# Values of two attention groups made once for eight heads with 512-column products, instead of twice for four heads with 256-column ones

## The chip, the cores and the metric

The kernel runs on one core of a Trainium2 chip. The metric is the device time of one launch in microseconds (us). All arithmetic is on fp32 data. TensorE (PE) multiplies, VectorE (DVE) and ScalarE (ACT) do the elementwise work, GpSimd (POOL) a little of it, and SyncE (SP) issues the DMAs between memory and SBUF.

## The reference, cut to what matters

There are 1024 tokens of width 1024 and two layers. Layer A is an mLSTM mixer. Layer B is dilated window attention with 8 heads of width 128 and three groups `g`, whose dilations are 1, 4 and 16; keys and values of all groups come from layer A's normalised output `x`.

```python
x = layer_norm(ALPHA * x + mlstm_layer(x, ...), ln_g[0], ln_b[0])
kv = (x @ w_kv).reshape(bsz, s, 2 * N_GROUPS_B, HEADS_B, HEAD_DIM_B)
for g, (window, dilation) in enumerate(GROUPS_B):       # (128,1), (512,4), (2048,16)
    kb, vb = blocks(kv[:, :, 2 * g]), blocks(kv[:, :, 2 * g + 1])
    o, lse = dilated_block_attention(qb, kb, vb, dilation, window // dilation, slopes)
wts = softmax(stack(lses), axis=0)
o = sum(wts[..., None] * stack(outs), axis=0)
y = (o * silu(z)) @ w_out
x = layer_norm(ALPHA * x + y, ln_g[1], ln_b[1])
```

The values of a group are `x` (1024 x 1024) times a 1024 x 1024 part of `w_kv`: 128 columns for each of the 8 heads.

## The kernel before

**Products.** An fp32 product is three TensorE matmuls over a high and a low part of each operand (`mm3`, lines 97, 98 and 99). `split` makes the parts: ACT casts the high one (L92), DVE subtracts it from the source for the low one (L93). Large products are Strassen's seven products of quarters. `operands` holds x in quarters "11", "12", "22" and sums "s1" to "s4", each made (by adds, L141) and split when it is first asked for. `strassen_steps` yields between its products, so that the caller can put other work there.

**Layer A's end.** The last output rows are normalised, transposed on TensorE (`transposes`, L1012) and evicted to SBUF with gain and shift (ACT at L1018, DVE at L1016). The last four of eight row blocks are handled by `self.a_last`, which `layer_b` calls inside its first product.

**Layer B.** Heads go in two quads, 0 to 3 and 4 to 7; for each quad the groups 0, 1, 2. For a quad and a group, `values` comes first, then for each head `queries_keys` (a Strassen product of 84 matmuls of 512 columns), `scores`, `head_values` (splits of the head's values) and `attend` (P times V). After group 2 a head's three outputs are merged: `merge` works out per-token weights in rows of 8 partitions (L1360 to L1379) and stores them as "f"; `fetch` loads the outputs and the weights broadcast to 128 partitions (tiles `fbs`); `weigh` calls `combine`, which multiplies and adds tiles of 128x1024 on DVE (L1401, L1403) and multiplies by the gate (L1405). `weigh` of a head runs after the next head's scores; that of head 3 runs inside `values(0, 1)` (argument `beside`).

**Values before.** For groups 0 and 1, `values(g, quad)` makes 4 heads' values, 512 columns. In `strassen_steps` with `tokens`, the stationary operand is 128 tokens of x and the moving one 256 columns of weights; one call is 7 products of 48 matmuls. For group 1 the result is regrouped by a store to memory ("vn") and a load. Group 2 is made in another way (`values_turned`).

**Gates.** `gates(c2)` makes silu gates for two heads of a layer-B column block, a Strassen product of 84 matmuls of 512 columns. `gates(0)` is interleaved with `values(0, 0)`; `gate_at` puts the others ahead of `values` of a (quad, group).

**Order.** A tile scheduler orders the instructions of each engine from the code's order, priorities and the slots (numbered SBUF buffers) that become free; on the chip each engine runs its list in that order.

## Time and profile before

| what | value |
| --- | --- |
| median of 3 runs | 2027.93 us (2026.33 to 2030.51) |
| profiled execution | 2026.42 us, its span from first to last instruction 2024.6 us |
| TensorE busy | 1975.5 us, 98% of the span |
| VectorE busy | 1453.3 us, 72% |
| ScalarE busy | 1014.2 us, 50% |
| mean granted TensorE clock | 0.994 of full speed |

Layer A takes the first 966 us of the span. A granted clock of 1.00 is the higher of TensorE's two levels (2.4 GHz), 0.50 the lower (1.2 GHz). Times within the program are us from the span's start. TensorE's instructions overlap in part, so the time that one adds is the distance between two starts, not its own duration.

### The profile page before, as it was taken

How to read it: one execution, taken by the hardware profiler on the slowest of the kernel's cores; microseconds unless marked ns; L12 is line 12 of the kernel's file. 1: busy time of each engine (PE TensorE's matmuls, PEld its weight loads, DVE VectorE, ACT ScalarE, POOL GpSimd, SP SyncE). 2: the span in 40 equal slices, each digit the busy share in tenths (PEclk: the TensorE clock that was granted, in tenths of full speed). 3: DMA queues.
4: the chain of work that ended last, by engine and by line, in shares of the span. 5: the costliest groups of instructions: out<-in, count | busy, mean ns of one | idle time of the engine just before them, and what ended most of it. 6: DMA issues, size and time to landing. Idle time of an engine off the chain costs nothing. (4 is left out here: it accounts for less than half of the span.)

```text
span 2024.6 us, 28010 instructions
## 1 busy us (share of the span) xinstructions
PE 1975.5 (98%) x10248; PEld 1671.0 (83%) x10248; DVE 1453.3 (72%) x2835; ACT 1014.2 (50%) x1976; POOL 153.3 (8%) x127
## 2 busy tenths in 40 slices
...
DMA packets 113025, 288.15 MB, mean 142 GB/s; under 512 B 13108, under 2 KB 35060, under 8 KB 112888
## 3 DMA queue, kind: packets, MB, share of 16 engines
...
HBM read 200.03 MB, written 86.30 MB: 141 GB/s over the span
## 5 line engine op out<-in xcount | busy, mean ns | idle before, releaser
L97 PE MATMUL b<-s,s 128*128 128x512 f32 (+2 forms) x2944 | 1065.1, 371 | 24.1 <-ACT s L92 20.6
L98 PE MATMUL b<-s,s 128*128 128x512 f32 (+2 forms) x2944 | 1077.7, 367 | 5.2 <-DVE s L93 5.2
L99 PE MATMUL b<-s,s 128*128 128x512 f32 (+2 forms) x2944 | 1063.9, 368 | 4.2 <-DVE s L93 4.1
L92 ACT CAST s<-s 128x512 fp32r<-128x512 f32 (+4 forms) x674 | 435.6, 660 | 534.8 <-PE b L99 276.2
L93 DVE TENSOR_TENSOR s<-s,s 128x512 fp32r<-128x512 f32 (+2 forms) x670 | 507.7, 770 | 250.0 <-ACT s L92 246.8
L97 PEld LDWEIGHTS b<-s,s 128*128 128x128 f32 x2944 | 556.7, 189 | 119.7 <-ACT s L92 27.2
L99 PEld LDWEIGHTS b<-s,s 128*128 128x128 f32 x2944 | 556.9, 190 | 95.5 <-DVE s L93 7.8
L98 PEld LDWEIGHTS b<-s,s 128*128 128x128 f32 x2944 | 557.6, 190 | 92.6 <-DVE s L93 6.8
L230 DVE TENSOR_TENSOR s<-s,b 128x512 f32<-128x512 f32 x168 | 114.6, 683 | 56.3 <-PE b L99 55.0
L1250 ACT ACTIVATE s<-s,nmax 128x128 f32<-128x128 f32 (+1 forms) x192 | 84.7, 444 | 34.4 <-DVE nmax L1248 34.1
L224 DVE TENSOR_TENSOR s<-s,b 128x512 f32<-128x512 f32 x112 | 76.4, 685 | 26.2 <-PE b L99 25.5
L93 DVE TENSOR_TENSOR s<-b,s 128x512 fp32r<-128x512 f32 (+1 forms) x96 | 51.0, 552 | 37.4 <-ACT s L92 33.8
L558 DVE SCALAR_TENSOR_TENSOR s<-s,c_convw,s 128x512 f32<-128x512 f32 (+3 forms) x96 | 71.6, 758 | 3.1 <-ACT s L555 2.8
L243 DVE TENSOR_TENSOR s<-s,s 128x512 f32<-128x512 f32 (+1 forms) x52 | 38.0, 731 | 44.3 <-DMA s<-in_w_xm 14.3
L802 ACT ACTIVATE s<-s,k 128x128 f32<-128x128 f32 x144 | 47.4, 395 | 40.7 <-DVE s L93 18.3
L1246 DVE CUSTOM_DVE_ANT_0 s<-b,k 128x128 f32<-128x128 f32 (+1 forms) x192 | 57.0, 345 | 7.0 <-PE b L99 6.8
L92 ACT CAST s<-b 128x512 fp32r<-128x512 f32 (+1 forms) x96 | 43.5, 481 | 23.9 <-PE b L99 14.2
L1197 DVE SCALAR_TENSOR_TENSOR s<-s,s 128x512 fp32r<-128x512 f32 x48 | 42.4, 885 | 14.7 <-ACT s L1196 14.4
L761 POOL TENSOR_TENSOR s<-s 128x512 fp32r<-128x512 f32 x32 | 43.3, 1365 | 77.1 <-DMA s<-dv 51.3
L872 POOL TENSOR_TENSOR s<-s,s 128x512 f32<-128x512 f32 x32 | 42.3, 1338 | 63.2 <-DVE s L871 51.3
L1326 ACT COPY s<-b 128x512 f32<-128x512 f32 x32 | 36.0, 1124 | 17.6 <-PE b L1287 9.1
L1401 DVE TENSOR_TENSOR s<-s,s 128x1024 f32<-128x1024 f32 (+1 forms) x27 | 29.3, 1103 | 21.5 <-DMA s<-df 21.3
...
## 6 DMA issues: line engine op xcount, KB each, us to landing
...
```

Source lines behind the costliest of these rows:

```text
L92: self.nc.scalar.copy(h, src)
L93: self.last_split = (l_eng or self.nc.vector).tensor_tensor(l, src, f(h), op=ALU.subtract)
L97: mm(ps, lh, rh, start=start, stop=False, skip_group_check=skip)
L98: mm(ps, lh, rl, start=False, stop=False, skip_group_check=skip)
L99: mm(ps, ll, rh, start=False, stop=stop, skip_group_check=skip)
L224: V.tensor_tensor(o, p, q, op=add)
L230: V.tensor_tensor(o, p[lane][rows], q[lane][rows], op=add)
L558: V.scalar_tensor_tensor(u[i][:, lo:o + 512], xm[i][:, lo - s:o + 512 - s], convw[:, c, 3 - s:4 - s], u[i][:, lo:o + 512], op0=ALU.mult, o ...
L761: G.tensor_tensor(l, f(l), f(h), op=ALU.subtract)
L802: A.activation(E[:, i * P:i * P + P], src[:, i * P:i * P + P], AF.Exp, bias=self.bias[:, hd, ig, j:j + 1])
L1246: V.tensor_tensor_reduce(out=dst, in0=sc, in1=bias, op0=ALU.add, op1=ALU.max, scale=1.0, scalar=-3e38, accum_out=mx[:, b:b + 1])
L1250: A.activation(res[b][0], res[b][0], AF.Exp, bias=nm[:, b:b + 1], accum_out=stat[:, 1, g, b:b + 1])
```

## The change

`values(g)` for g = 0 and 1 runs once, at quad 0, for all 8 heads, with `strassen_wide`: the moving operand is 512 columns wide and a result quarter holds 4 heads. A call is again 7 products of 48 matmuls. The half for heads 0 to 3 stays in SBUF; that for heads 4 to 7 is stored to "vn" and loaded at quad 1. For group 1 both halves are regrouped through "vn". `head_values` splits four pieces of 256 columns instead of two of 512. `gates(0)` moves ahead of `values(1, 0)` and `gates(2)` from ahead of `values(1, 1)` to the start of quad 1. `operands` gets spare slots for "s2", and `values(0)` asks for "s2" and "s3" behind the first product and `a_last`. `transposes` takes the columns in another order and `a_last` other PSUM banks. The combine of head 3 is no longer one `weigh` beside values but three steps of `by_group`, one behind the scores of each of heads 4, 5 and 6 of group 0. Only layer B's weights `w_v` are laid out anew for this; the output is the same sum.

```diff
@@ -955,7 +955,7 @@
         lnT = self.const("lnT", [P, 2, KD])
         self.x1 = self.operands(raws, {"11": (4, 5, 6, 7), "12": (8, 9, 10, 11), "22": (0, 1, 2, 3),
                                        "s1": (16, 17, 18, 19), "s2": (20, 21, 22, 23), "s3": (24, 25, 26, 27),
-                                       "s4": (28, 29, 30, 31)}, {})
+                                       "s4": (28, 29, 30, 31)}, {}, spare=(30, 31))
         rs = Ring(44, 45, 46, 52, 13, 47, 48, 49)
         w_raw, whs, wls, yhl = Ring(50, 51), Ring(47, 0, 1, 34), Ring(40, 2, 3, 36), Ring(41, 42, 43, 35)
         rows, stats = {}, {}
...
@@ -1062,7 +1062,7 @@
                     norm((tb - 2, tb - 1, tb))
                 elif i == 3:
                     norm((tb,))
-        self.a_last = lambda: [transposes((4, 5, 6), Ring(2, 3, 4, 5)), transposes((7,), Ring(6, 7))]
+        self.a_last = lambda: [transposes((4, 5, 6), Ring(4, 5, 6, 7)), transposes((7,), Ring(4, 5, 6, 7))]
     def layer_b(self):
@@ -1093,50 +1093,66 @@
             return (dst.rearrange("p (r h i) -> p r h i", r=r, h=2)[:, :, half],
                     src.rearrange("p (i r) -> p r i", r=r))
-        def values(g, quad, beside=None):
+        def values(g, quad):
             if g == 2:
                 return values_turned(quad)
-
-            s0, s1, s2, s3 = vs
-            slots = {(0, 0): s2, (1, 0): s0, (1, 1): s3, (0, 1): s1}
-            vs[:] = s2, s0, s3, s1
-            v = [[None, None], [None, None]]
+            rows = lambda quad, half: self.dram["vn", g, quad, half]
+            natural = lambda ap: ap.rearrange("(t p) n -> p t n", p=P)
+
+            grouped = natural if g == 0 else lambda ap: ap.rearrange("(p r) n -> p r n", r=4)
+            v = [None, None]
+
+            def load(half):
+                for j, t in enumerate(v[half]):
+                    nc.sync.dma_start(t, grouped(rows(quad, half))[:, 2 * j:2 * j + 2])
+
+            if quad:
+                for half in range(2):
+                    v[half] = [self.slot(i, (P, 2, 512)) for i in vs[2 * half:2 * half + 2]]
+                    load(half)
+                return v
+            to = {}
+
+            places = {(0, 0): vs[2:4] if g == 0 else vs[0:2], (1, 0): vs[0:2] if g == 0 else vs[2:4],
+                      (1, 1): (48, 49) if g == 0 else (36, 37), (0, 1): (44, 45)}
             def place(half, i):
-                v[half][i] = t = self.slot(slots[half, i])
-                return [[(t[:, 512 * lane:512 * lane + 512], slice(0, P))] for lane in range(2)]
+                to[half, i] = [self.slot(n, (P, 2, 512)) for n in places[half, i]]
+                return [t[:, j] for t in to[half, i] for j in range(2)]
             def done(half, i, aps):
                 if half + i == 0:
-                    for ap, [(o, _)] in zip(aps, place(0, 0)):
+                    for o, ap in zip(place(0, 0), aps):
                         A.copy(o, ap)
-                if g == 1:
-
-                    t, rows = v[half][i], self.dram["vn", quad, half, i]
-                    nc.sync.dma_start(rows.rearrange("(t p) n -> p t n", p=P), t.rearrange("p (t n) -> p t n", t=4))
-                    nc.sync.dma_start(t.rearrange("p (r n) -> p r n", r=4), rows.rearrange("(p r) n -> p r n", r=4))
-
-            self.w_raw = Ring(38, 39, s0, s1) if g + quad else Ring(44, 45, 46, 52)
-            b11, b21, b12, b22 = self.quarters(a["w_v"][g, quad])
-            steps = self.strassen_steps((b11, b12, b22, b21), x, ((0, 1), (2, 3), (4, 5), (6, 7)), place, done, V,
-                                        early=not g + quad, tokens=lambda ap, t: ap[:, t * P:t * P + P])
-            if not g + quad:
-
-                next(steps)
+                if i == 0:
+                    v[half] = to[half, i]
+                if i or g:
+                    for j, t in enumerate(to[half, i]):
+                        nc.sync.dma_start(natural(rows(i, half))[:, 2 * j:2 * j + 2], t)
+                if g and i == 0:
+                    load(half)
+
+            raw = {}
+            for n, slots in zip((0, 3, 1, 2), ((44, 45), (46, 52), (28, 29), (50, 51)) if g == 0 else
+                                ((38, 39), (44, 45), (46, 47), (52, 15))):
+                kh, nh = ((0, 0), (0, 1), (1, 1), (1, 0))[n]
+                raw[n] = [self.slot(i) for i in slots]
+                for j in range(2):
+                    nc.sync.dma_start(raw[n][j], a["w_v"][g, kh, nh, j])
+            u_slots, self.u_slots = self.u_slots, Ring(43, 12, 13, 47) if g == 0 else Ring(43, 12, 48, 49)
+            steps = self.strassen_wide([raw[n] for n in range(4)], x, ((0, 1, 2, 3), (4, 5, 6, 7)), place, done, V)
+            next(steps)
+            if g == 0:
+
                 self.a_last()
-                next(steps)
-                self.w_raw, u_slots, self.u_slots = Ring(50, 51), self.u_slots, Ring(13)
-                ahead = gates(0, (47, 48), ((7,), (1,), (2,), (3,)))
-                next(ahead), next(ahead)
-                self.u_slots = u_slots
+                x["s2"], x["s3"]
             for n, _ in enumerate(steps):
-                if beside and n == 1:
-                    beside()
-            if not g + quad:
-                for _ in ahead:
-                    pass
+                if g == 0 and n == 3:
+                    x["22"], x["s4"]
+            self.u_slots = u_slots
+            if g == 0:
                 gain0.extend(self.ln_params(0, 50, 51))
             return v
@@ -1166,12 +1182,14 @@
             if g == 2:
                 return [(None, v[hh][:, b * P:b * P + P]) for b in range(8)]
-            i, cs = hh // 2, slice(P * (hh % 2), P * (hh % 2) + P)
+            cs = slice(P * hh, P * hh + P)
             h, l = [self.slot(s, (P, 2, 4, P), F32R) for s in vhl]
             for half in range(2):
-                self.split(h[:, half], l[:, half], v[half][i].rearrange("p (t n) -> p t n", t=4)[:, :, cs])
+                for j in range(2):
+                    ts = slice(2 * j, 2 * j + 2)
+                    self.split(h[:, half, ts], l[:, half, ts], v[half][j][:, :, cs])
             at = lambda b: (b // 4, b % 4) if g == 0 else (b % 2, b // 2)
-            whole = lambda half, t: v[half][i].rearrange("p (t n) -> p t n", t=4)[:, t, cs]
+            whole = lambda half, t: v[half][t // 2][:, t % 2, cs]
             return [(h[:, at(b)[0], at(b)[1]], l[:, at(b)[0], at(b)[1]], whole(*at(b))) for b in range(8)]
         def queries_keys(h, g):
@@ -1405,6 +1423,31 @@
                     V.tensor_tensor(acc[:, cs], acc[:, cs], z[:, cs], op=ALU.mult)
             return acc
+        def by_group(h, acc, o, fb):
+
+            tiles = {}
+
+            def load(g):
+                tiles[g] = self.slot(o if g else acc), self.slot(fb)
+                nc.sync.dma_start(tiles[g][0], self.dram["og", h, g])
+                nc.sync.dma_start(tiles[g][1], self.dram["f", h][g:g + 1, :].to_broadcast([P, SEQ]))
+
+            def step(g):
+                t, acc = tiles[g][0], tiles[0][0]
+                V.tensor_tensor(t, t, tiles[g][1], op=ALU.mult)
+                if g:
+                    V.tensor_tensor(acc, acc, t, op=ALU.add)
+                if g < 2:
+                    load(g + 1)
+                    return
+                z = self.slot(fb)
+                nc.sync.dma_start(z, self.dram["z2", h])
+                V.tensor_tensor(acc, acc, z, op=ALU.mult)
+                nc.sync.dma_start(self.dram["y2", h], acc)
+
+            load(0)
+            return step
+
         def weigh(h, fetched):
             with self.tc.issue_after(self.last_split.ins):
@@ -1436,7 +1479,7 @@
         works, late = Ring(36), None
         fbs = Ring(49, 51, 52)
-        gate_at = {(0, 2): 1, (1, 1): 2}
+        gate_at = {(0, 1): 0, (0, 2): 1, (1, 0): 2}
         for quad in range(2):
             heads = range(4 * quad, 4 * quad + 4)
             accs, os = (Ring(44, 15), Ring(15, 44))[quad], Ring(37, 46, 50)
@@ -1447,15 +1490,16 @@
                     self.w_raw = raw2
                     for _ in gates(gate_at[quad, g], qk_slots):
                         pass
-                beside = None
-                if late and g == 0:
-                    beside, late = (lambda part=late: weigh(*part)), None
-                v = values(g, quad, beside)
+                v = values(g, quad)
                 for h in heads:
                     qk = queries_keys(h, g)
                     p = scores(h, g, qk, stats[h])
-                    if late:
+                    if late and g == 2:
                         y6, late = weigh(*late), None
+                    if (quad, g) == (1, 0) and h < 7:
+
+                        with self.tc.issue_after(self.last_split.ins):
+                            fourth(h - 4)
                     if g == 2:
                         if h == 7:
                             works = 44
@@ -1465,7 +1509,9 @@
                         residual(4 + h)
                     if g == 2:
                         merge(h, *fac)
-                        if h < 6:
+                        if h == 3:
+                            fourth = by_group(h, 50, 51, 52)
+                        elif h < 6:
                             late = h, fetch(h, accs, os, fbs)
                         elif h == 6:
                             late = h, (*fetch(h, accs, os, fbs, False)[0:2], None)
```

`strassen_wide`, which the change calls, is in the kernel already; layer A uses it:

```python
def product(acc, w, xp, first):
    for k in range(4):
        wh, wl = self.pair(self.w_hl)
        self.split(wh, wl, w[k // 2][:, k % 2 * 512:k % 2 * 512 + 512], eng)
        xh, xl = [p[k // 2][:, k % 2] for p in xp]
        for t in range(4):
            ts = slice(t * P, t * P + P)
            self.mm3(acc[t], xh[:, ts], xl[:, ts], wh, wl, first and k == 0, k == 3, skip=True)
```

**Three places in the order.** First TensorE's list in the first product of `values(0)`, at layer A's end; a row is line, operation, output from inputs (b a PSUM bank, s a slot of SBUF), partitions by columns. Before:

```order
L99 MATMUL b_1456_8365<-s_1488_8499,s_1389_7957 128x256
L97 MATMUL b_1456_8365<-s_1488_8499,s_1388_7956 128x256
L98 MATMUL b_1456_8365<-s_1488_8499,s_1388_7956 128x256
L99 MATMUL b_1456_8365<-s_1488_8499,s_1389_7957 128x256
L97 MATMUL b_1456_8365<-s_1488_8499,s_1388_7956 128x256
L98 MATMUL b_1456_8365<-s_1488_8499,s_1388_7956 128x256
```

And of the change:

```order
L97 MATMUL b_1464_8377<-s_1502_8535,s_1388_7956 128x512
L98 MATMUL b_1464_8377<-s_1502_8535,s_1388_7956 128x512
L99 MATMUL b_1464_8377<-s_1502_8535,s_1389_7957 128x512
L97 MATMUL b_1464_8377<-s_1503_8550,s_1388_7956 128x512
L98 MATMUL b_1464_8377<-s_1503_8550,s_1388_7956 128x512
L99 MATMUL b_1464_8377<-s_1503_8550,s_1389_7957 128x512
```

The same triple of matmuls now covers 512 columns, and a bank holds one block of 128 tokens instead of two halves of two.

Second VectorE's list at layer A's end, behind the eviction of the last transposes. Before, where s_1511 is a low part of "s2" and L93 of 128x512 are low parts of weights:

```order
L93 TENSOR_TENSOR s_1507_8639<-s_1453_8359,s_1507_8639 128x512
L243 TENSOR_TENSOR s_1548_9039<-s_1549_9041,s_1548_9039 128x512
L93 TENSOR_TENSOR s_1523_8804<-s_1356_7767,s_1522_8803 128x1024
L93 TENSOR_TENSOR s_1513_8705<-s_1452_8357,s_1513_8705 128x512
L93 TENSOR_TENSOR s_1531_8874<-s_1362_7793,s_1530_8873 128x1024
L141 TENSOR_TENSOR s_1359_7780<-s_1477_8462,s_1359_7780 128x1024
L141 TENSOR_TENSOR s_1365_7806<-s_1365_7806,s_1477_8462 128x1024
L93 TENSOR_TENSOR s_1511_8675<-s_1477_8462,s_1510_8674 128x1024
L1426 SCALAR_TENSOR_TENSOR s_1491_8556<-s_1491_8556,b_1495_8562 128x512
L93 TENSOR_TENSOR s_1512_8678<-s_1452_8357,s_1512_8678 128x512
L93 TENSOR_TENSOR s_1518_8743<-s_1454_8361,s_1518_8743 128x512
L93 TENSOR_TENSOR s_1525_8808<-s_1359_7780,s_1524_8807 128x1024
```

And of the change, where s_1475 and s_1481 are quarter "22" of x, s_1492 and s_1493 the sum "s2" (L151), s_1495 and s_1497 its low parts:

```order
L93 TENSOR_TENSOR s_1537_8820<-s_1475_8452,s_1536_8819 128x1024
L93 TENSOR_TENSOR s_1501_8528<-s_1478_8463,s_1500_8527 128x1024
L141 TENSOR_TENSOR s_1356_7767<-s_1492_8511,s_1356_7767 128x1024
L141 TENSOR_TENSOR s_1359_7780<-s_1359_7780,s_1492_8511 128x1024
L151 TENSOR_TENSOR s_1493_8513<-s_1481_8474,s_1478_8463 128x1024
L93 TENSOR_TENSOR s_1495_8516<-s_1492_8511,s_1494_8515 128x1024
L93 TENSOR_TENSOR s_1539_8824<-s_1481_8474,s_1538_8823 128x1024
L243 TENSOR_TENSOR s_1564_8987<-s_1565_8989,s_1564_8987 128x512
L93 TENSOR_TENSOR s_1529_8752<-s_1356_7767,s_1528_8751 128x1024
L141 TENSOR_TENSOR s_1362_7793<-s_1493_8513,s_1362_7793 128x1024
L141 TENSOR_TENSOR s_1365_7806<-s_1365_7806,s_1493_8513 128x1024
L93 TENSOR_TENSOR s_1497_8520<-s_1493_8513,s_1496_8519 128x1024
```

The sums and splits of x stand in another order, and, counted from the first sum (L141) behind the transposes, the two low parts of "s2" come behind ten and fifteen rows of 128x1024.

Third VectorE's list where quad 1 begins; before, in `queries_keys` of head 4:

```order
L230 TENSOR_TENSOR s_2161_13324<-s_2142_12918,b_2140_12916 128x512
L1401 TENSOR_TENSOR s_2120_12885<-s_2120_12885,s_2123_12888 128x1024
L230 TENSOR_TENSOR s_2161_13324<-s_2142_12918,b_2141_12917 128x512
L93 TENSOR_TENSOR s_2175_13373<-s_2166_13331,s_2175_13373 128x512
L1401 TENSOR_TENSOR s_2121_12886<-s_2121_12886,s_2124_12889 128x1024
L1403 TENSOR_TENSOR s_2119_12884<-s_2119_12884,s_2120_12885 128x1024
L93 TENSOR_TENSOR s_2176_13389<-s_2167_13333,s_2176_13389 128x512
L1403 TENSOR_TENSOR s_2119_12884<-s_2119_12884,s_2121_12886 128x1024
L93 TENSOR_TENSOR s_2189_13517<-s_2148_13030,s_2188_13516 128x512
L93 TENSOR_TENSOR s_2189_13517<-s_2158_13267,s_2188_13516 128x512
L260 TENSOR_TENSOR s_2167_13333<-s_2167_13333,s_2166_13331 128x512
L1405 TENSOR_TENSOR s_2119_12884<-s_2119_12884,s_2125_12890 128x1024
```

And of the change, where L1421 and L1423 are `combine` of head 2 (L1403 and L1405 before), the rows of 8x128 and 8x384 `merge` of head 3, the 128x256 rows the first four splits of `head_values`, and the last row a low part of weights for `queries_keys` of head 4 (rows left out between 8x128 and 128x512 are more of the merge):

```order
L1421 TENSOR_TENSOR s_2149_12850<-s_2149_12850,s_2151_12852 128x1024
L1381 TENSOR_TENSOR s_2178_13035<-s_2178_13035 8x128
L1423 TENSOR_TENSOR s_2149_12850<-s_2149_12850,s_2155_12856 128x1024
L1381 TENSOR_TENSOR s_2178_13035<-s_2178_13035 8x128
L1386 TENSOR_TENSOR s_2178_13035<-s_2178_13035 8x384
L1469 SCALAR_TENSOR_TENSOR s_2191_13098<-s_2191_13098,b_2197_13106 128x512
L93 TENSOR_TENSOR s_2242_13441<-s_2209_13238,s_2241_13440 128x256
L93 TENSOR_TENSOR s_2242_13441<-s_2210_13239,s_2241_13440 128x256
L93 TENSOR_TENSOR s_2242_13441<-s_2211_13242,s_2241_13440 128x256
L93 TENSOR_TENSOR s_2242_13441<-s_2212_13243,s_2241_13440 128x256
L224 TENSOR_TENSOR s_2223_13258<-s_2223_13258,b_2220_13255 128x512
L93 TENSOR_TENSOR s_2227_13308<-s_2218_13252,s_2227_13308 128x512
```

Before, `combine` of head 3 (L1401, L1403, L1405) stood among the weight splits; now `combine` of head 2, the merge of head 3 and four value splits stand ahead of such a split.

## Rows read from the trace of the kernel before

**Rows 1.** The page, its first lines: busy us (share of the span), instructions.

```profile
span 2024.6 us, 28010 instructions
...
PE 1975.5 (98%) x10248; PEld 1671.0 (83%) x10248; DVE 1453.3 (72%) x2835; ACT 1014.2 (50%) x1976; POOL 153.3 (8%) x127
```

**Rows 2.** Groups by line and shape, TensorE: busy us, mean ns, idle before.

```profile
L97 PE MATMUL b<-s,s 128*128 128x512 f32 x2224 | 863.5, 396 | 20.6 <-ACT s L92 17.1 <-DVE s L230 2.5 <-ACT s L1193 0.6
...
L97 PE MATMUL b<-s,s 128*128 128x256 f32 x648 | 187.1, 292 | 3.4 <-ACT s L92 3.4
```

**Rows 3.** Timeline of TensorE, two stretches, first and last: start us, duration us.

```profile
1166.28 0.28 PE L97 MATMUL b<-s,s 128*128 128x256 f32 x1
...
1186.44 0.40 PE L97 MATMUL b<-s,s 128*128 128x512 f32 x1
...
1189.18 0.39 PE L97 MATMUL b<-s,s 128*128 128x512 f32 x1
...
1197.34 0.39 PE L97 MATMUL b<-s,s 128*128 128x512 f32 x1
```

**Rows 4.** Windows: from:to, length, busy us per engine (instructions), granted clock, DMA.

```profile
966.00:1012.00 46.00, 38.65 (x270) 36.14 (x269) 40.31 (x63) 28.54 (x42) 0.00 (x0) 0.93 0.16 64
986.20:989.60 3.40, 3.40 (x9) 2.65 (x8) 3.40 (x4) 1.87 (x2) 0.00 (x0) 0.50 0.07 27
1436.00:1516.00 80.00, 73.80 (x503) 67.28 (x502) 65.86 (x121) 31.31 (x59) 0.00 (x0) 0.98 0.49 172
1040.00:1110.00 70.00, 70.00 (x356) 59.59 (x355) 51.12 (x113) 35.67 (x83) 0.00 (x0) 1.00 0.17 61
```

**Rows 5.** TensorE's waits, 966 to 1012: total us, times, longest us.

```profile
PE b L98 <- DVE s L93: 3.7, 1, 3.7
PE b L97 <- ACT s L92: 2.8, 2, 2.3
```

**Rows 6.** Timeline of VectorE, 976 to 1010.

```profile
980.12 1.23 DVE L141 TENSOR_TENSOR s<-s,s 128x1024 f32<-128x1024 f32 x1 [0.73 <-ACT s L1018]
...
987.05 1.23 DVE L141 TENSOR_TENSOR s<-s,s 128x1024 f32<-128x1024 f32 x1
988.18 1.23 DVE L93 TENSOR_TENSOR s<-s,s 128x1024 fp32r<-128x1024 f32 x1
...
993.86 0.70 DVE L93 TENSOR_TENSOR s<-s,s 128x512 fp32r<-128x512 f32 x1
994.46 0.69 DVE L243 TENSOR_TENSOR s<-s,s 128x512 f32<-128x512 f32 x1
```

**Rows 7.** Timeline of TensorE, 1496 to 1510.

```profile
1500.55 0.39 PE L99 MATMUL b<-s,s 128*128 128x512 f32 x1
1504.30 0.50 PE L97 MATMUL b<-s,s 128*128 128x512 f32 x1 [3.37 <-ACT s L92]
```

**Rows 8.** Timeline of VectorE, 1440 to 1486.

```profile
1457.53 0.94 DVE L1375 RECIPROCAL s<-s 8x128 f32<-8x128 f32 x1
1458.50 0.89 DVE L1379 TENSOR_TENSOR s<-s 8x128 f32<-8x128 f32 x3
...
1465.35 1.23 DVE L1401 TENSOR_TENSOR s<-s,s 128x1024 f32<-128x1024 f32 x1 [2.11 <-DMA s<-df]
1466.93 1.22 DVE L1401 TENSOR_TENSOR s<-s,s 128x1024 f32<-128x1024 f32 x1 [0.35 <-DMA s<-df]
...
1483.41 0.86 DVE L1379 TENSOR_TENSOR s<-s 8x128 f32<-8x128 f32 x3
```

**Rows 9.** Groups by line and shape, VectorE.

```profile
L93 DVE TENSOR_TENSOR s<-s,s 128x512 fp32r<-128x512 f32 x572 | 402.2, 710 | 209.7 <-ACT s L92 206.8 <-PE b L1264 1.2
...
L93 DVE TENSOR_TENSOR s<-b,s 128x256 fp32r<-128x256 f32 x48 | 19.4, 417 | 4.3 <-ACT s L92 4.2
```

**Rows 10.** Timeline of SyncE's queue, 1186 to 1215: when a DMA was issued.

```profile
1187.35 0.37 SPq L1118 DMA_DIRECT2D dn<-s  x1
1190.32 0.32 SPq L1119 DMA_DIRECT2D s<-dn  x1
```

14 lines of the change are left out of this document (7 added, 7 removed).

## Prediction

> **What bounds the kernel.** I read the page's busy shares first: TensorE is busy 98% of a span of 2024.6 us [rows 1], so the time is TensorE's own work plus its few stops, and an edit counts as far as it shortens either. The groups by line say what the work is: almost all of it lies in triples of matmuls of 512 and of 256 columns, and their idle time is small [rows 2]. A busy engine hides that its instructions overlap, so I took the price of one from the timeline, as the distance between starts in a dense stretch: from 1166.28 to 1186.44 there are 168 matmuls of 256 columns, 0.1200 us each, and from 1189.18 to 1197.34 there are 36 of 512, 0.2267 us each [rows 3]. Then I cut the span into windows. In a head stage TensorE is busy all of 70 us while VectorE has 51.1 us of work, so VectorE has room there. Two windows lose time: layer A's end (46.0 us, 38.65 busy) and the change of quads (80.0 us, 73.80 busy) [rows 4]. In both, the long stops of TensorE end with a weight cast of ACT or a split of VectorE [rows 5, 7], and in both VectorE runs full-width sums without a break, one of 128x1024 every 1.13 us and one of 128x512 every 0.60 us [rows 6]. A stop of over 2 us is followed by 3.4 us at granted clock 0.50 [rows 4], the lower level (1.2 GHz), in which a matmul takes twice its time; half of 3.4 us, 1.7 us, is lost. Layer A's end has two such stretches and so loses 7.35 + 3.4 = 10.8 us; the change of quads has one and loses 6.2 + 1.7 = 7.9 us.
>
> **The change, part by part.**
>
> *Merged products.* Before, four calls of 7 products of 48 matmuls, 1344 of 256 columns. Now two calls, 672 of 512 columns. Each pair costs 0.2400 before and 0.2267 after, 13.3 ns less; times 672 that is **-9.0 us**. The Trainium skill ("TensorE: Matmul & The Clock Gate", section Back-to-back issue gap) gives the gap as the column count at 2.4 GHz plus about 2.5 ns; by that the pair saves 2.5 ns, 1.7 us in all. The trace does not agree: both distances lie above the rule's (109 and 216 ns), and the narrow one by more.
>
> *Splits, casts, sums of the values.* The number and size of weight splits and result adds over all heads stay the same; a call has 28 low parts and 30 sums and adds of 512 columns, 58 x 0.6 = 35 us of VectorE beside 336 x 0.2267 = 76 us of TensorE. Nothing. `head_values` now makes four pieces of 256 instead of two of 512, in 16 (head, group) stages: 32 more instructions on each of ACT and VectorE. On VectorE two of 417 ns replace one of 710 [rows 9], 32 x 0.12 = 4 us over the kernel, in head stages with 18.9 us of room in 70 [rows 4]. Hidden; if that cover is gone, up to 4 us. I take 0.5.
>
> *Transfers.* The halves for heads 4 to 7 add 4 MB of stores and loads in 512 KB pieces. A store of this kind is followed by its dependent load 2.97 us later [rows 10]; the loads are issued when head 3's last products give up the slots, and VectorE's list comes to them some 12 us later (below), so they are hidden by the gates' products. Nothing, with the rival below.
>
> *Layer A's end.* Ahead of the product with "s2" TensorE now has two products of 48 matmuls at 0.2267 us and 32 transposes at no more than 0.12: from 966 that is 25.6 us, to 991.5. On VectorE the first sum behind the transposes stood at 980.12 [rows 6]; the transposes now start behind 36 matmuls of 512 (8.2 us) instead of 48 of 256 (5.8 us), so I put it at 982.5. From it to the first low part of "s2" the list has 11 rows of 1024 (1.14 us), 2 of 512 (0.6) and 2 evictions of 128 columns (I take 0.33): 14.4 us, so 996.9. TensorE can do 8 matmuls with the high part and stops at 993.3: 3.6 us. The second low part comes 6.3 us later, at 1003.2, where TensorE, with 24 matmuls (5.4 us) to do, asks for it at 1002.3: 0.9 us. With one slow-clock stretch the loss is 6.2 us. If ACT's evictions hold VectorE up as they did once before (0.73 us [rows 6]) at several of its steps, up to 5 us come on top. Between 6.2 and 11.2 I take 8.8, against 10.8: **-2 us** (bounds -4.6 and +0.4).
>
> *Change of quads.* Before, `combine` of head 3 held VectorE among the weight splits (L1401 to L1405), and TensorE stopped from 1500.55 to 1504.30 [rows 7]. That goes: `by_group` spreads the same rows over three heads with room. But `values(0, 1)` goes too, 40 us of TensorE's work that covered `combine` of head 2 and the merge of head 3; now only the gates cover them. Take TensorE's L1351 of head 3 (the transpose of its statistics) as 0. From it to the second half of the gates' first bank stand 50 matmuls of 512 and 13 small ones, taken at 0.12: 50 x 0.2267 + 13 x 0.12 = 12.9 us. That half needs the weight split that is the last row of VectorE's third excerpt. VectorE: the weights of head 2 are stored behind L1397 (L1379 before), which ends some 3.3 us ahead of 0; the first product with a loaded weight (L1419, before L1401) came 6.0 us behind that end before (1459.4 to 1465.35 [rows 8]), so now at 2.7. The same `combine` and merge took 1465.35 to 1484.3 before [rows 8], 18.9 us, with 11 rows of 512 between; 5 stand between now, so 18.9 - 6 x 0.6 = 15.3. Behind it come one L1469, four value splits, one add and the split itself: 0.6 + 4 x 0.35 + 0.6 + 0.6 = 3.2. It is done at 21.2, 8 us late. With one slow-clock stretch and some 1.5 us of small stops that the window has anyway, the loss is 11 us, against 7.9: **+3 us**. Bounds: if VectorE's merge is early enough, only the wait for the slot is left, some 1.4 us, and the window gains 5; if the merge's loads come late too, it loses 4 more.
>
> *The other moved pieces.* `gates(0)` and `gates(2)` are 84 matmuls of 512 columns at either place. Spare slots, banks and the transposes' order add no instruction.
>
> **Sum.** -9.0 + 0.5 - 2 + 3 = -7.5 us: the profiled execution goes from 2026.42 to about 2018.9. The median of the runs is 1.5 us above that execution, so 2027.93 - 7.5 = **2020.4 us**. About 0.2%, 4.1 us, is what a measurement of this kernel can tell from no change; that puts the limits at 2023.9 and 2032.0.
>
> **The rivals.**
>
> *The stop at the change of quads does not come.* For it: VectorE's head stages have room [rows 4], so merge and `combine` may run ahead. Against: the loads of the weights set the earliest start. The window then loses some 3 us instead of 11: 2020.4 - 8 = 2012.
>
> *The new waits eat the gain.* For it: both windows hang on VectorE's order, and 7.5 us are little against two stops with a slow clock each. At the upper bounds of both (+2.4 and +4) and with the extra splits not hidden (+3.5) it comes to 2030: no change that can be told.
>
> *The merged step costs what two cost.* If what spaces the narrow steps now (their operands, their banks) and not their number sets the pace, a step of 512 columns takes 0.24 us, the first term is nothing and the time 2029.4. The distances of 0.2267 in rows speak against it [rows 3]. By the rule on the issue gap the first term would be 1.7 us and the time 2027.7.
>
> *Slower: the values of heads 4 to 7 come back late.* VectorE's list has their four splits ahead of the weight splits of `queries_keys`, so a late load holds everything behind it. The list comes to them 12 us after the loads can be issued; to pass 2032 a load must cost 11.6 us more than that, so land some 24 us after its issue, eight times the 2.97 us of a store [rows 10]. Each further us costs one: 30 us give 2038.
>
> *The wide calls do not run dense* (operands late in every product): against it, layer A's wide and narrow products run dense now. It would come to 2024 to 2030.
>
> **How the numbers follow.** Chances: forecast 0.50 (its own range 2016 to 2024), no stop at the change of quads 0.22, waits eat the gain 0.17, merged step without saving or not dense 0.03, late values 0.08. The range 2011 to 2027 leaves out the late values, half of the third case and a little below. Faster by over 0.2%: 0.50 less a tail, and 0.22, 0.71 together; within 0.2%: 0.20; slower: 0.09.
>
> **What the profile after would show.** Right: 672 fewer records on L97 to L99 in the values, distances of 0.227 us there and no stop inside the two calls; TensorE's busy time 9 us lower; at layer A's end one or two stops on VectorE's splits of "s2", 8 to 9 us lost; at the start of quad 1 one stop of about 8 us on a weight split behind L1397, with a slow-clock stretch behind it; no stop on L1437 to L1445. Wrong: distances of 0.24, a stop on the loads of "vn", or idle time at the change of quads well under 5 or over 15 us.

## The result

The changed kernel is slower. Its median is 2031.92 us (2030.45 to 2036.85, 12 runs) against 2027.54 us for the kernel before on the same chips (12 runs): a ratio of 1.0027, 95% interval 1.0018 to 1.0035, some 5.5 us. The forecast was 2020.4 us, 7.5 us faster, with a range that ended at 2027.

### The profile after

The page of the changed kernel, its first lines, beside [rows 1]:

```profile
span 2030.0 us, 26710 instructions
...
PE 1969.2 (97%) x9576; PEld 1633.7 (80%) x9576; DVE 1450.0 (71%) x2867; ACT 1011.9 (50%) x2008; POOL 155.1 (8%) x127
```

There are 672 matmuls fewer and TensorE is busy 6.3 us less, yet the span is 5.4 us longer, so its idle time grew by 11.7 us. The groups by line and shape say whom it waited for (busy us, mean ns of one, then idle time before them and what ended it), beside [rows 2]:

```profile
L98 PE MATMUL b<-s,s 128*128 128x512 f32 x2448 | 961.6, 393 | 0.5 <-DVE s L93 0.5
L99 PE MATMUL b<-s,s 128*128 128x512 f32 x2448 | 949.1, 394 | 8.2 <-DVE s L93 7.8
L97 PE MATMUL b<-s,s 128*128 128x512 f32 x2448 | 939.0, 396 | 36.9 <-ACT s L92 28.8 <-DVE s L230 7.7 <-DVE s L871 0.2
```

The first matmul of a triple lost 20.6 + 3.4 us before in its two widths [rows 2] and loses 36.9 now, and 28.8 of that end with a cast of ACT. A cast takes some 0.6 us; in the two longest stops, below, it was late because its own input, or a row ahead of it in ACT's list, was late.

The timeline of TensorE (start us, duration us) at the first and the last of 260 matmuls of `values(1)`:

```profile
1200.81 0.39 PE L98 MATMUL b<-s,s 128*128 128x512 f32 x1
...
1259.51 0.39 PE L99 MATMUL b<-s,s 128*128 128x512 f32 x1
```

58.70 us over 259 distances is 0.2266 us each, the distance of 512 columns before [rows 3]: the merged products run dense at the pace that the first term took.

The two windows that the prediction turned on, with their later places in the new program, and the heads of group 1 (from:to, length, then busy us and instructions of each engine, granted clock, DMA share, GB/s), beside [rows 4]:

```profile
966.00:1012.00 46.00, 38.51 (x170) 30.92 (x169) 37.35 (x60) 28.51 (x44) 0.00 (x0) 0.89 0.15 58
1510.00:1590.00 80.00, 66.12 (x307) 52.90 (x306) 62.54 (x123) 33.94 (x66) 0.00 (x0) 0.94 0.53 177
1287.30:1387.30 100.00, 96.21 (x503) 80.01 (x502) 75.91 (x189) 64.51 (x161) 0.00 (x0) 1.00 0.31 111
```

The same 100 us from the first scores of group 1 on, in the kernel before:

```profile
1214.00:1314.00 100.00, 98.22 (x521) 83.38 (x520) 80.71 (x191) 67.05 (x160) 0.00 (x0) 1.00 0.33 116
```

Layer A's end has about the idle time that it had (38.65 us busy before), but a granted clock of 0.89 in place of 0.93. The change of quads lost: 13.9 us idle where 6.2 were. And in the heads of group 1, where the prediction saw only hidden work, 100 us hold 18 matmuls fewer. Their idle time differs by 2.0 us only. A matmul of 512 columns is recorded for 0.39 us and the next one starts after 0.227, so a delay of up to some 0.16 us shows no idle time at all, and there the count tells more than the busy share. (A trace can lack records, but the changed kernel with splits of 512 columns, below, shows 521 again.)

**Layer A's end.** TensorE's timeline (in brackets the idle time before and what ended it):

```profile
992.31 0.49 PE L1012 MATMUL b<-c_ident,s 128*128 128x128 f32 x3
997.35 0.50 PE L97 MATMUL b<-s,s 128*128 128x512 f32 x1 [4.56 <-ACT s L92]
...
999.85 0.63 PE L98 MATMUL b<-s,s 128*128 128x512 f32 x1
1003.41 2.08 PE L99 MATMUL b<-s,s 128*128 128x512 f32 x4 [2.93 <-DVE s L93]
```

and VectorE's, beside [rows 6]; L151 makes the two parts of the sum "s2":

```profile
988.86 1.22 DVE L141 TENSOR_TENSOR s<-s,s 128x1024 f32<-128x1024 f32 x1
...
995.00 1.23 DVE L151 TENSOR_TENSOR s<-s,s 128x1024 f32<-128x1024 f32 x1
996.13 0.41 DVE L1016 TENSOR_SCALAR s<-b,c_lnT 128x128 f32<-128x128 f32 x1
996.46 2.35 DVE L93 TENSOR_TENSOR s<-s,s 128x1024 fp32r<-128x1024 f32 x2
...
1001.00 1.22 DVE L151 TENSOR_TENSOR s<-s,s 128x1024 f32<-128x1024 f32 x1
```

The last transposes before:

```profile
981.97 0.44 PE L1012 MATMUL b<-c_ident,s 128*128 128x128 f32 x2 [0.55 <-ACT s L1018]
```

Now the last transposes (L1012) end at 992.8, since in TensorE's list they stand between the matmuls of the second wide product, and VectorE comes to the last eviction (L1016) at 996.13 only. The first part of "s2" starts at 995.00, behind rows that VectorE has run without a pause since 985.81, and the first stop ends with its cast; the second part starts at 1001.00, behind the last eviction, and the second stop ends with its low part.

**The change of quads.** Here TensorE has one long stop:

```profile
1555.89 0.39 PE L99 MATMUL b<-s,s 128*128 128x512 f32 x1
1565.26 0.80 PE L97 MATMUL b<-s,s 128*128 128x512 f32 x1 [8.98 <-ACT s L92]
```

ACT's timeline tells why the cast was late:

```profile
1559.31 0.60 ACT L1468 ACTIVATE s<-b 128x512 f32<-128x512 f32 x1 [2.36 <-DMA dy<-s]
1559.81 0.62 ACT L1468 ACTIVATE s<-s 128x512 f32<-128x512 f32 x1
1562.89 1.32 ACT L92 CAST s<-s 128x256 fp32r<-128x256 f32 x4 [2.46 <-DMA df<-s]
1564.12 0.57 ACT L237 COPY s<-b 128x512 f32<-128x512 f32 x1
1564.60 0.62 ACT L92 CAST s<-s 128x512 fp32r<-128x512 f32 x1
```

And the queue of SyncE says when the two stores were issued, the second one behind the last rows of head 3's merge on VectorE:

```profile
1555.24 0.32 SPq L1456 DMA_DIRECT2D dy<-s  x1
...
1561.40 0.29 SPq L1398 DMA_DIRECT2D df<-s  x1
```

```profile
1560.55 0.82 DVE L1397 TENSOR_TENSOR s<-s 8x128 f32<-8x128 f32 x3
```

The cast that TensorE needs is the last of these five rows. Ahead of it ACT waited twice, each time for a store to give up a slot: the gate columns of `gates(2)` (L1468, a tanh) go into slot 44, out of which head 2's merged rows (dy) were being stored, and the high parts of head 4's values go into slot 36, out of which head 3's weights (df) were being stored.

### The profile page after: what moved, and what is told of

It reads as the page before. It is cut to its first block, busy times and chain, and to the rows that moved or that the text cites. A ratio compares the mean times of both kernels' runs of the same rounds, so it can differ in the third digit from the quotient of the medians.

```text
span 2030.0 us, 26710 instructions
## 1 busy us (share of the span) xinstructions
PE 1969.2 (97%) x9576; PEld 1633.7 (80%) x9576; DVE 1450.0 (71%) x2867; ACT 1011.9 (50%) x2008; POOL 155.1 (8%) x127
## 4 chain that ended last, share of the span: by engine, by line
PE 77%; DVE 12%; DMA 6%; ACT 3%; issue 2%; SPq 0%; DVEq 0%; ACTq 0%
PE b L97 24%; PE b L99 24%; PE b L98 23%; DVE s L93 3%; PE b L593 1%; DMA s<-in_w_qk 1%; PE b L1282 1%; ACT s L92 1%; DMA s<-df 1%; DMA s<-in_w_out 1%; DVE s L230 1%; DVE s L1419 1%; PE b L599 1%; PE b L868 1%; DVE s L1421 1%
## 5 line engine op out<-in xcount | busy, mean ns | idle before, releaser
L97 PE MATMUL b<-s,s 128*128 128x512 f32 (+2 forms) x2720 | 1013.9, 387 | 36.9 <-ACT s L92 28.8
L98 PE MATMUL b<-s,s 128*128 128x512 f32 (+3 forms) x2720 | 1037.9, 383 | 1.2 <-DVE s L93 1.2
L99 PE MATMUL b<-s,s 128*128 128x512 f32 (+3 forms) x2720 | 1024.4, 383 | 8.2 <-DVE s L93 7.8
L93 DVE TENSOR_TENSOR s<-s,s 128x512 fp32r<-128x512 f32 (+3 forms) x702 | 511.5, 743 | 285.9 <-ACT s L92 280.6
L92 ACT CAST s<-s 128x512 fp32r<-128x512 f32 (+3 forms) x706 | 437.7, 637 | 543.8 <-PE b L99 279.6
L97 PEld LDWEIGHTS b<-s,s 128*128 128x128 f32 x2720 | 513.1, 189 | 141.9 <-ACT s L92 36.0
L99 PEld LDWEIGHTS b<-s,s 128*128 128x128 f32 x2720 | 512.2, 189 | 110.1 <-DVE s L93 13.9
L98 PEld LDWEIGHTS b<-s,s 128*128 128x128 f32 x2720 | 513.5, 189 | 97.4 <-DVE s L93 2.9
L230 DVE TENSOR_TENSOR s<-s,b 128x512 f32<-128x512 f32 x144 | 98.1, 682 | 34.8 <-PE b L99 33.5
L224 DVE TENSOR_TENSOR s<-s,b 128x512 f32<-128x512 f32 x96 | 65.4, 684 | 17.3 <-PE b L99 13.8
L93 DVE TENSOR_TENSOR s<-b,s 128x512 fp32r<-128x512 f32 (+1 forms) x96 | 51.6, 553 | 33.2 <-ACT s L92 29.4
L243 DVE TENSOR_TENSOR s<-s,s 128x512 f32<-128x512 f32 x48 | 33.1, 690 | 52.5 <-DMA s<-in_w_qk 19.3
L314 DVE TENSOR_TENSOR s<-s,b 128x512 f32<-128x512 f32 x80 | 50.9, 681 | 7.5 <-PE b L99 5.7
L310 DVE TENSOR_TENSOR s<-s,s 128x1024 f32<-128x1024 f32 x32 | 40.1, 1253 | 17.8 <-DMA s<-in_w_o 9.9
```

The source lines that it names most:

```text
L92: self.nc.scalar.copy(h, src)
L93: self.last_split = (l_eng or self.nc.vector).tensor_tensor(l, src, f(h), op=ALU.subtract)
L97: mm(ps, lh, rh, start=start, stop=False, skip_group_check=skip)
L98: mm(ps, lh, rl, start=False, stop=False, skip_group_check=skip)
L99: mm(ps, ll, rh, start=False, stop=stop, skip_group_check=skip)
L224: V.tensor_tensor(o, p, q, op=add)
```

## The experiments

All ratios are to the kernel before on the same chip, with their 95% interval. A gain over the change is the difference of two such ratios, the change's own being 1.0027, so each gain is uncertain by some 2.7 us either way (an estimate from the two intervals). Stops are given as TensorE's idle time, like the 8.98 us above. The expectations have them by the distance of starts, 0.1 to 0.4 us longer (9.1 us for the 8.98), and their "7.3 us stop" is two stops together. The timeline shows neighbours; only an edit shows which of them holds the others.

**Pieces alone.** The kernel before with nothing but the four splits of 256 columns in `head_values`:

```diff
-                self.split(h[:, half], l[:, half], v[half][i].rearrange("p (t n) -> p t n", t=4)[:, :, cs])
+                for j in range(2):
+                    ts = slice(2 * j, 2 * j + 2)
+                    self.split(h[:, half, ts], l[:, half, ts],
+                               v[half][i].rearrange("p (t n) -> p t n", t=4)[:, ts, cs])
```

> The kernel before with one thing of the change: head_values splits four pieces of 256 columns instead of two of 512. Theory P (the pieces cost VectorE and ACT their room in the heads of group 1, where the change lost 4.3 us in quad 0 and 2.7 us in quad 1): 3 to 5 us slower than before, about 2031.5, the loss in the group-1 heads. Rival S (those losses come from the new order of the list, not from the pieces): within 1.5 us of before.

Measured: 1.0028 (1.0016 to 1.0040), 5.7 us for an edit that the prediction put at 0.5, somewhat more than theory P's 3 to 5. The 100 us of group 1 hold 499 matmuls here, 22 fewer than before:

```profile
1216.70:1316.70 100.00, 95.64 (x499) 79.20 (x498) 74.88 (x187) 63.81 (x159) 0.00 (x0) 1.00 0.32 110
```

The two kernels have the same number of matmuls, 10248, so the n-th of one can be set beside the n-th of the other. When group 1 of heads 0 to 3 starts (1214 us in the kernel before) the kernel with the pieces is 2.7 us late, at 1377 us 7.9, and at 1880 us, behind the last of the pieces, 8.7: of the 6.1 us lost in that time, 5.3 lie in and right behind this one group. (The first 2.7 us come from layer A, which the edit doesn't touch.)

**The pieces everywhere but in group 1 of heads 0 to 3** (24 of the 32 additional splits):

```diff
+        slot_quad = [0]
...
+                if g and not slot_quad[0]:
+                    self.split(h[:, half], l[:, half], v[half][i].rearrange("p (t n) -> p t n", t=4)[:, :, cs])
+                    continue
...
+            slot_quad[0] = quad
```

> The kernel before with the values' splits in pieces of 256 columns everywhere except in group 1 of the first four heads (24 of the 32 additional splits). Theory (the pieces cost only where TensorE stops for a split behind them in the list, which the trace shows in group 1 of heads 0 to 3 alone): ratio to before 0.9995 to 1.0008. Rival (each piece costs alike, some 5.7 us over 32): 4.3 us, ratio 1.0021.

Measured: 1.0008 (0.9996 to 1.0019). The theory's range ends at this value, and the rival's 1.0021 lies just outside the interval; by the ratios alone the margin is small. Set matmul by matmul beside the kernel before, this one is 0.65 us late at 1214 us, 2.6 at 1377 and 2.9 at 1880. Of the 2.0 us in group 1, where it has no pieces, 1.7 are half of a stretch of 3.4 us at granted clock 0.50 (1259.3 to 1262.7 us), which the kernel before does not have there:

```profile
1214.60:1314.60 100.00, 97.86 (x512) 82.94 (x511) 79.48 (x189) 66.01 (x157) 0.00 (x0) 0.98 0.33 116
```

So the 24 pieces elsewhere cost next to nothing in this trace, and the 8 in group 1 of heads 0 to 3 carry most of the 5.7 us. It isn't the price of a piece.

**Values read back for two heads at once** (the changed kernel; the loads bring 256 columns of all four row blocks, so a split covers 512 again, except in group 0 of heads 0 to 3):

```diff
-                for j, t in enumerate(v[half]):
-                    nc.sync.dma_start(t, grouped(rows(quad, half))[:, 2 * j:2 * j + 2])
+                for i, t in enumerate(v[half]):
+                    nc.sync.dma_start(t, grouped(rows(quad, half))[:, :, 256 * i:256 * i + 256])
...
+                if paired:
+                    self.split(h[:, half], l[:, half], v[half][i][:, :, ps])
+                    continue
```

> The changed kernel with values that come through memory (all but group 0 of heads 0 to 3) loaded as tiles of two heads and four token blocks, so that head_values splits two pieces of 512 there again. Theory P (the four pieces cost what b_quarters showed, above all in group 1 of quad 0): 3 to 6 us faster than the change, a ratio to before of 0.9995 to 1.001, and the stage of group 1 in quad 0 loses 3 us less. Rival S (only the order of the list matters there): within 1.5 us of the change, ratio 1.002 to 1.003.

Measured: 1.0004 (0.9994 to 1.0015), 4.7 us less than the change, as theory P had it. Matmul by matmul 4.3 us of gain come between 1300 and 1400 us, in group 1 of heads 0 to 3, which is back at 521 matmuls:

```profile
1287.50:1387.50 100.00, 98.22 (x521) 83.38 (x520) 80.75 (x191) 66.96 (x160) 0.00 (x0) 1.00 0.33 116
```

VectorE's timeline shows what the pieces moved. In the changed kernel:

```profile
1328.01 0.69 DVE L243 TENSOR_TENSOR s<-s,s 128x512 f32<-128x512 f32 x1 [1.98 <-DMA s<-in_w_qk]
1328.62 0.68 DVE L230 TENSOR_TENSOR s<-s,b 128x512 f32<-128x512 f32 x1
```

and with 512 columns a split:

```profile
1325.81 0.69 DVE L230 TENSOR_TENSOR s<-s,b 128x512 f32<-128x512 f32 x1 [1.42 <-PE b L99]
1327.80 0.69 DVE L243 TENSOR_TENSOR s<-s,s 128x512 f32<-128x512 f32 x1 [1.30 <-DMA s<-in_w_qk]
```

The scheduler put a weight sum that waits for its load (L243) ahead of the add (L230) that frees TensorE's bank, 2.8 us later than without pieces, and TensorE stopped 1.43 us for that add, at 1329.36. The kernel with the pieces alone has the same two rows in the same order. This is the longest stop; the others of the stretch are of at most 0.6 us.

**Head 3's weights in another work slot** (15 for 36, so that `head_values` doesn't wait for their store):

```diff
                         if h == 7:
                             works = 44
+                        elif h in (3, 4):
+                            works = 15 if h == 3 else Ring(36)
```

> The changed kernel with the merge rows of head 3 in another SBUF slot, so that ACT's four value casts of head 4 no longer wait for the merge's store. Theory L (VectorE's list is what holds the weight split at the change of quads): the 9.1 us stop shrinks by the casts' wait only, to about 7, the time falls by 1.5 to 2.5 us to about 2029.5. Rival A (ACT's wait on the store is what holds it): the stop shrinks to 2 us or less and the time falls by 8 or more, to 2023.

Measured: 1.0011 (1.0002 to 1.0021). The stop of 9.0 us became two of 5.0 and 1.7, and one of 1.9 stands some 14 us earlier, where the change has 0.6. The slot of the merge's store is a part of it, more than theory L gave it and less than rival A, not the whole.

**Head 3's merge behind head 4's scores** (with slot 15 too; the steps of `by_group` move on by a head):

```diff
-                    if (quad, g) == (1, 0) and h < 7:
+                    if (quad, g) == (1, 0) and h == 4:
+                        merge(3, *fac)
+                        fourth = by_group(3, 50, 51, 52)
+                    elif (quad, g) == (1, 0):
                         with self.tc.issue_after(self.last_split.ins):
-                            fourth(h - 4)
+                            fourth(h - 5)
...
-                        merge(h, *fac)
+                        if h != 3:
+                            merge(h, *fac)
...
```

> The changed kernel with the merge of head 3 called behind the scores of head 4, and the three combine steps of head 3 behind the scores of heads 4 (its loads only), 5, 6 and 7. Theory L: the merge's rows (about 6 us) and the wait on its store leave VectorE's list ahead of the weight split; only the combine of head 2 is left there: the 9.1 us stop shrinks to 2 or 3, the slow-clock stretch behind it may go too, 6 to 9 us faster than the change, about 2024. Rival C (the combine of head 2 and its loads alone hold the split): the stop stays over 7, the time within 2 us of the change.

Measured: 1.0010 (1.0000 to 1.0021), stops of 5.0 and 1.7 us, as with slot 15 alone; both expectations missed. The code was moved, the list wasn't: in VectorE's list the merge still stood ahead of the weight splits. So this run says nothing on the merge beyond the slot, and the next ties it.

**The merge tied behind head 4's last weight split:**

```diff
...
+                        with self.tc.issue_after(self.last_split.ins):
+                            merge(3, *fac)
...
```

> As a_merge_late, but the merge rows of head 3 are tied behind the last weight split of queries_keys of head 4, so that VectorE's list really has them behind the split that TensorE waits for. Theory L (the list ahead of that split sets the stop): 4 to 5 us of merge rows go from ahead of it, the 7.3 us stop of a_merge_late shrinks to 2 to 4, 4 to 6 us faster than a_merge_late, ratio to before 0.998 to 0.999. Rival C (the loads and the combine of head 2 hold it): the stop stays over 6, ratio 1.001.

Measured: 1.0003 (0.9992 to 1.0013), slower than theory L forecast, with a stop below the rival's 6 us. The long stop is 4.6 us, 9.0 in the change, and one of 2.6 stands ahead of it. With the merge out of the way TensorE still stopped, and VectorE's gate row waited 3.31 us for ACT's tanh.

**Both (values for two heads at once, and the merge tied), with `head_values` of head 4 tied behind that split as well:**

```diff
+                    with self.tc.issue_after(self.last_split.ins) if (quad, g, h) == (1, 0, 4) else ExitStack():
+                        hv = head_values(g, v, h % 4)
...
```

> Both edits, and the value splits of head 4 tied behind the weight splits too. If the two causes are apart, the gains add: 9 to 12 us faster than the change, ratio to before 0.9965 to 0.9985, faster than both kernels. If one of them only uncovers the other stop, the ratio is 0.999 to 1.000.

Measured: 0.9981 (0.9971 to 0.9991), faster than both kernels and in the range for gains that add. A stop of 6.1 us stayed, and ACT's timeline shows what holds it:

```profile
1559.40 0.60 ACT L1474 ACTIVATE s<-b 128x512 f32<-128x512 f32 x1 [7.71 <-DMA dy<-s]
```

The tanh of the gate columns (L1474 in this kernel) waited 7.71 us for the store of head 2's rows, now that neither the merge nor the slot of `head_values` stood in the way.

**The gates back in their old place** (`gates(2)` ahead of group 1 of quad 1):

```diff
-        gate_at = {(0, 1): 0, (0, 2): 1, (1, 0): 2}
+        gate_at = {(0, 1): 0, (0, 2): 1, (1, 1): 2}
```

> The changed kernel with gates(2) back ahead of group 1 of quad 1. Theory L: at the change of quads the product of 84 matmuls that covers VectorE's list is now queries_keys of head 4 itself, with the same list ahead of its splits, so the stop is 8 to 11 us again, and what follows it (scores and attend of head 4) has no product beside it: 0 to 5 us slower than the change, 2032 to 2037. Rival G (the gates at this place are what brings the stop): the stop is under 4 us and the time under 2027.

Measured: 1.0004 (0.9994 to 1.0013), 4.7 us less than the change. Theory L fell: it had a long stop again and no gain. The rival fits better: the 9.0 us stop is gone. But stops of 3.2 and 3.8 us come in head 4's products, ahead of which the gates' 84 matmuls no longer stand.

**The gate columns in other slots**, the change otherwise untouched:

```diff
-                    for _ in gates(gate_at[quad, g], qk_slots):
+                    for _ in gates(gate_at[quad, g], (45, 47)):
```

> The changed kernel with layer B's second pair of gate columns in other work slots, so that their result doesn't wait for the store of head 2's rows. Theory (the stop at the change of quads has several causes of nearly the same length, the merge rows of head 3 and the slots they share with head_values besides the store): alone this gains at most 2 us, ratio to before 1.0017 to 1.0030, and a stop of 7 to 9 us stays at the change of quads. Rival (the store alone holds the gate columns, and they alone hold TensorE): a gain of 5 us or more, ratio 1.000 or below, and the stop under 4 us.

Measured: 0.9969 (0.9958 to 0.9981). My theory fell and the rival holds: this one line takes back the whole loss and more. The window of the change of quads and TensorE's waits in it (total us, times, longest us):

```profile
1510.00:1590.00 80.00, 74.26 (x356) 60.55 (x355) 69.39 (x146) 38.62 (x80) 0.00 (x0) 0.98 0.57 197
```

```profile
PE b L97 <- DVE s L230: 2.5, 1, 2.5
PE b L97 <- ACT s L92: 2.3, 3, 1.1
PE b L99 <- DVE s L93: 1.0, 1, 1.0
```

74.3 us busy where the change had 66.1, and the longest wait is 2.5 us where it was 9.0. The scheduler's list follows the slots. The tanh that waited for the store in the change, the only one of the four rows at L1468 that reads a bank (`s<-b`), runs 21 us earlier here:

```profile
1538.39 0.58 ACT L1468 ACTIVATE s<-b 128x512 f32<-128x512 f32 x1
```

ACT's weight casts at 1553.96, 1558.47 and 1561.59 now stand between the rows of head 3's merge, not behind them: the merge's last rows (L1397) run at 1570.77, those of the change at 1560.55. The store and the merge end some 2 us apart in the change (1559.3 and 1561.4), which is why I took them for causes of equal weight; but with the gate columns free to run early, the splits came ahead of the merge's last rows by themselves. So the one edit moved two things, the wait for the store and the place of the merge in VectorE's list; which share each has of the gain is not shown, only that the slot number is enough to bring both.

By the spans of the two profiled executions the gain is 5.9 us, by the ratios 11.8; the profiled one lies 2.4 us above this kernel's median. Matmul by matmul it is 9.4 us from 1700 us on and next to nothing up to 1510, so it lies at the change of quads; 3.5 of it go again between 1885 and 1925 us, where the stops of the two executions differ; whether the edit has a part in that is not shown.

**The last transposes ahead of the second wide product** (three quarters of that product tied behind them):

```diff
-                for t in range(4):
-                    ts = slice(t * P, t * P + P)
-                    self.mm3(acc[t], xh[:, ts], xl[:, ts], wh, wl, first and k == 0, k == 3, skip=True)
+                with self.tc.issue_after(self.last_t.ins) if hold and k else ExitStack():
+                    for t in range(4):
+                        ts = slice(t * P, t * P + P)
+                        self.mm3(acc[t], xh[:, ts], xl[:, ts], wh, wl, first and k == 0, k == 3, skip=True)
```

> The changed kernel with layer A's last transposes tied ahead of three quarters of the second wide product of values(0). Theory T (the product with s2 is late because the last transposes stand behind matmuls that are now twice as wide, so that VectorE's first sum starts at 988.9 and not near 982): that sum starts 3 to 5 us earlier, the two stops of 4.8 and 3.3 us shrink to 4 together, 3 to 5 us faster than the change. Rival E (evictions and the norm of the last row block set the sums' start, and TensorE waits for the transposes instead): the stops move ahead of the transposes and the time stays within 1.5 us.

Measured: 0.9994 (0.9984 to 1.0005), 6.7 us less than the change by the ratios, 4.1 by the spans. Theory T had the gain and the place, not the row: the first sum comes 1.7 us earlier (987.17 for 988.86), not 3 to 5. What moved is the eviction of the last transposes, from 996.13 to 989.45, and with it both parts of "s2" (L151), from 995.00 and 1001.00 to 990.90 and 993.17. The first stop is gone and the second, 3.3 us here, stays:

```profile
989.45 0.40 DVE L1017 TENSOR_SCALAR s<-b,c_lnT 128x128 f32<-128x128 f32 x1
...
990.90 1.22 DVE L151 TENSOR_TENSOR s<-s,s 128x1024 f32<-128x1024 f32 x1
...
993.17 1.22 DVE L151 TENSOR_TENSOR s<-s,s 128x1024 f32<-128x1024 f32 x1
```

```profile
966.00:1012.00 46.00, 41.92 (x188) 33.27 (x187) 39.29 (x65) 28.96 (x45) 0.00 (x0) 0.96 0.15 58
```

**All cures together** (values in pairs, transposes first, and):

```diff
...
+                        elif h in (3, 4):
+                            works = 15 if h == 3 else Ring(36)
...
+                        with self.tc.issue_after(self.last_split.ins):
+                            merge(3, *fac)
...
-                    for _ in gates(gate_at[quad, g], qk_slots):
+                    for _ in gates(gate_at[quad, g], (45, 47)):
```

> All the cures together on the changed kernel: values read back for two heads at once (splits of 512 columns), last transposes of layer A ahead of the second wide product, head 3's rows in another slot and with head_values behind the last weight split, gate columns in other slots. Theory (four separate losses that lie in different stretches): the gains add, ratio to before 0.993 to 0.995, 2014 to 2018 us, with no stop over 4 us at the change of quads and the stops at layer A's end at most 4 us. Rival (the gains overlap, another wait takes the place of each): ratio 0.998 or above.

Measured: 0.9956 (0.9940 to 0.9971), just above the theory's range and well below the rival's 0.998. The longest stop at the change of quads is 3.0 us, at layer A's end 3.35.

**Three cures, head 3's merge left as the change has it** (values in pairs, transposes first, gate slots):

```diff
...
-                    nc.sync.dma_start(t, grouped(rows(quad, half))[:, 2 * j:2 * j + 2])
+                    nc.sync.dma_start(t, grouped(rows(quad, half))[:, :, 256 * i:256 * i + 256])
...
-            steps = self.strassen_wide([raw[n] for n in range(4)], x, ((0, 1, 2, 3), (4, 5, 6, 7)), place, done, V)
+            steps = self.strassen_wide([raw[n] for n in range(4)], x, ((0, 1, 2, 3), (4, 5, 6, 7)), place, done, V, hold=g == 0)
...
-                    for _ in gates(gate_at[quad, g], qk_slots):
+                    for _ in gates(gate_at[quad, g], (45, 47)):
```

> Three cures on the changed kernel and head 3's rows left as the change has them: values read back for two heads at once, last transposes ahead of the second wide product, gate columns in other slots. Theory (with the store's slot out of the way the rows of head 3 hold nothing, so their move in the kernel with all cures was worth nothing): ratio to before 0.993 to 0.996, no stop over 3 us at the change of quads. Rival (the move of head 3's rows was worth its share): ratio 0.998 or above and a stop over 4 us at the change of quads.

Measured: 0.9950 (0.9937 to 0.9962), 2018.68 us, 10 us below the kernel before and the fastest here, with no stop over 2.5 us at the change of quads, as the theory had it. Moving the merge was worth nothing that these intervals can tell once the store's slot was free. The page of this kernel:

```profile
span 2018.2 us, 26665 instructions
...
PE 1968.8 (98%) x9576; PEld 1635.5 (81%) x9576; DVE 1450.4 (72%) x2843; ACT 1010.1 (50%) x1984; POOL 154.3 (8%) x127
```

Its span is 11.8 us below the change's. The spans of the three single cures are 2.1, 4.1 and 5.9 us below it, 12.1 together. That these add up proves little, since executions of one kernel scatter by more than that: those of the gate slots run from 2021.3 to 2029.1 us. By the ratios the cures would add to 0.9913, less than measured, and matmul by matmul the slots alone gain 9.5 us at the change of quads but some 6 on top of the other two cures. So the gains overlap in part, as far as these traces tell; by how much stays open.

## Why the prediction was wrong, point by point

| term | predicted us | measured us | from |
| --- | --- | --- | --- |
| merged products | -9.0 | -9.0 | 672 x (0.2400 - 0.2266) |
| pieces in `head_values` | +0.5 | +5.7 | pieces alone, 1.0028 |
| layer A's end | -2 | +0.4 | window: 7.49 idle + 3.66, against 10.75 |
| change of quads | +3 | +9.1 | window: 13.88 idle + 3.17, against 7.9 |
| sum | -7.5 | +6.2 | the ratio gives +5.5, the spans +5.4 |

The lost time of a window is its idle time and half of TensorE's busy time at granted clock 0.50, as in the prediction. At layer A's end the clock was at 0.50 for one stretch of 10.2 us, which spans the second stop; at the change of quads for two, of which the first began while TensorE stood still:

```profile
998.15:1008.39 10.24, 7.31 (x18) 5.23 (x17) 10.24 (x10) 5.49 (x9) 0.00 (x0) 0.50 0.08 31
1561.35:1568.18 6.83, 2.92 (x7) 2.25 (x8) 5.44 (x12) 3.15 (x8) 0.00 (x0) 0.50 0.47 155
1578.42:1581.83 3.41, 3.41 (x9) 2.64 (x8) 2.03 (x4) 0.00 (x0) 0.00 (x0) 0.50 0.00 0
```

Half of 7.31 us is 3.66; half of 2.92 + 3.41 us is 3.17. The sum's nearness to the ratio is not a test of each term: the pieces were measured on another kernel, with an interval of 2.4 us either way, and the two windows in one execution each.

**The merged products.** Right, in mechanism and size. Of the two prices the trace's held: the distance is 0.2266 us, and the rivals by which wide steps keep the pace of 0.24 or don't run dense are out. TensorE's busy time fell by 6.3 us, not by the 9 that the prediction named as a sign; where the rest went is not shown. The formula that the prediction took from the Trainium skill ("TensorE: Matmul & The Clock Gate", section Back-to-back issue gap) is given there for a single matmul by itself, not for a stream of weight loads and matmuls like this one; by it the term would have been 1.7 us. The distances in this kernel, dense for 59 us, say 9.0.

**The pieces.** The step that failed is "Hidden; if that cover is gone, up to 4 us. I take 0.5." The price of a piece was about right: four in a row take 1.39 us of VectorE at 1563.33, 0.35 each, so two cost 0.1 us more than one split of 512 columns (0.60). The argument was that VectorE's mean room in a stage, 18.9 us in 70, hides them. But the stop here hangs on the order in the list, not on the mean: in group 1 the additional rows turned an order in which a wait for a weight load stood behind TensorE's next need into one in which it stood ahead. Shown by edits, and by where their traces fall behind: that the pieces cost this, that group 1 of the first four heads carries most of it, and that wider splits take it back. That the order of L243 and L230 is the reason is read from the trace, not tried by itself, and it is one stop of several.

**Layer A's end.** The place and the two stops were right; the step that failed is "the transposes now start behind 36 matmuls of 512 (8.2 us) instead of 48 of 256 (5.8 us), so I put it at 982.5". The first sum came at 988.86. I moved the first transposes by 2.4 us, but what "s2" needs is the last ones, which stand between matmuls of double width and ended 10 us later than before (992.8). The stops are 4.6 and 2.9 us, not 3.6 and 0.9, and the slow-clock stretch was 10.2 us long, not 3.4. The +0.4 is the far bound that the text gave (-4.6 to +0.4); tying the transposes ahead takes the first stop away.

**The change of quads.** The one stop "of about 8 us on a weight split" came, in its place, 9.0 us long, and it ends with a cast for that split. What failed is its cause and what came with it. That the length came out near 8 is luck in part: the merge's rows, which the text counted, end at 1561.4, and the store that it did not count gave up its slot 2 us earlier. The text counted VectorE's rows up to the split and called the merge late; the edits show that the merge's code can stay where it is, and that the slot of a store holds the gate's tanh on ACT, with the casts behind it. "Now only the gates cover them" named the gates as cover and did not ask where they put their result; the wait for a slot stands only in a bound, at some 1.4 us. The other stops of the window make 4.9 us instead of 1.5, and there are two slow-clock stretches instead of one: together the +9.1 in place of +3.

**The rivals.** The new waits that eat the gain were the right kind, at 0.17, priced at 2030 with an upper bound of 4 us more at the change of quads, where it came to 6.1 more. The values of heads 4 to 7 did not come back late: of the idle time ahead of the splits of 256 columns, loads from memory ended 0.6 us in all.

```profile
L93 DVE TENSOR_TENSOR s<-s,s 128x256 fp32r<-128x256 f32 x72 | 30.9, 465 | 19.2 <-ACT s L92 18.5 <-DMA dn<-s 0.6
```

The three failed terms erred the same way: each priced the work, where the order of a list or a slot set most of the cost.
